# A three-block network on one core: 2 MB weight transfers in the second mixture, other queues and order in block 3

## The chip, the cores and the metric

The kernel runs on one core of one Trainium2 chip, in one launch. The metric is device time in microseconds (us), from the start to the end of one execution. Of the kernel before there are three timed runs and one profiled execution.

## The reference

Three blocks run one after the other on 512 tokens of 1024 features, in float32. Each has attention layers and then a mixture of experts or a feed-forward layer. The change touches the expert layer of block 2 and the mixer of block 3. In block 2 each of 16 experts takes the 64 tokens that score highest for it and applies a gated layer of width 2048:

```
def expert_choice_ffn(h, w_router, w_gate, w_up, w_down):
    cap = max(1, EC_FACTOR * s // N_EXPERTS_2)          # 64
    aff = jax.nn.softmax(logits, axis=-1)
    g, idx = lax.top_k(jnp.swapaxes(aff, 1, 2), cap)
    xe = h[bidx, idx]
    a = jnp.einsum('becd,edf->becf', xe, w_gate)        # 16 x [1024, 2048]
    u = jnp.einsum('becd,edf->becf', xe, w_up)          # 16 x [1024, 2048]
    ye = jnp.einsum('becf,efd->becd', jax.nn.silu(a) * u, w_down)   # 16 x [2048, 1024]
    ye = ye * g[..., None].astype(ye.dtype)
    return jnp.zeros_like(h).at[bidx, idx].add(ye)
```

So 16 experts have 24 MB of weights each, 384 MB in all (MB is 2^20 bytes here). Block 3 mixes two attentions, gated:

```
def hybrid_mixer_3(x, w_in, b_gate, ...):
    q_na, k_na, v_na, q_lat, kv_lat, k_rope, g_a, g_b = jnp.split(x @ w_in, offs, axis=-1)
    y_a = neighbourhood_attention_2d(q_na, k_na, v_na, na_rpb) @ w_branch_na
    y_b = latent_attention(q_lat, kv_lat, k_rope, ...) @ w_branch_mla
    merged = jax.nn.sigmoid(g_a + b_a) * y_a + jax.nn.sigmoid(g_b + b_b) * y_b
    return merged @ w_out
```

Both attentions have 8 heads; the latent one (MLA) attends over all 512 tokens, in four blocks of 128 queries.

## The kernel before

The kernel is written in a tile language: the program allocates tiles from pools, and a planner at build time orders each engine's instructions, queues included, by a simulated time line and puts in the waits. A pool with n buffers of a name hands them out in rotation, and a new use waits for the last reader of the old one. DMAs are issued from the queue of the engine named in the call: `nc.sync` is SyncE (SP in the profile), `nc.scalar` ScalarE (ACT), `nc.gpsimd` GpSimd (POOL). An engine's queue is worked off in order.

**The second mixture** (`moe2`, from line 1622). `lend` (line 330) builds a rotation of sixteen 1 MB buffers, [128, 2048] float32 each: 4 of the pool `rx`, the two halves of the tile `xl`, the 4 buffers `raw`, and 6 of the pool of the mixture (`rx` and the mixture's own are called `rawx` in the profile). `raw_tile` (line 323) hands out the next one; `raw_group` (line 349) issues the load on SyncE's queue (line 354). While the tokens are being chosen (line 1632), the first expert's weights are loaded as far as there is room, and three more blocks of its up matrix go into tiles that are idle then (line 1680).

Per expert, `gather` (line 1653) first collects the 64 tokens by matmuls with a one-hot matrix, for two experts at once: it writes `xe`, 8 blocks of 128 features. Then come gate and up: for each block k of 128 rows one load of 1 MB, in which each partition holds one row of 8 KB, and 4 matmuls of 512 columns (line 1701; each is two instructions in the trace). The product is transposed by TensorE (line 1726), with columns picked at a stride of 2 that matches how the down weights lie: 8 loads of 1 MB (line 1734), each partition with two neighbouring rows, 8 KB in one run, and the matmuls of line 1738. For each pair of experts the results go back to the tokens (line 1747).

**Block 3** (`mixer3`, from line 1789). The input arrives transposed and split in a high and a low part (`xh`, `xl`). `wsplit` casts each weight block on ScalarE (`wh`, line 227) and subtracts on VectorE (`wl`, line 230); each product is then three matmuls (lines 376 and 428). The values of the neighbourhood attention come first (`dense_tiles`): `ev_v` copies each of the four token tiles into the one buffer `nv` and stores it to memory (`vd`, line 1811). After queries and keys the windows of values are loaded back (`vw`, eight loads, line 1830), and per pair of heads two table rows (`rv`, line 1839). Stores, reloads and table rows are issued on ScalarE's queue. The weights for values, queries and keys come through the 4 `raw` buffers. `merged` are eight tiles for the gated sum, not yet in use at that time.

MLA comes in parts: a pair of heads `hp` and a block of queries `qt`. A part computes the scores of its two heads (line 1968), their softmax (`softmax2`), then transposes both (`transposes`, line 442), copies them out (lines 445 and 447) and multiplies with the values (line 1980), whose matmuls `together` keeps side by side. `stagger` (line 116) interleaves the parts: the second half of a part follows the first half of the next one (the first four parts) or of the second next (the other twelve).

Of the kernel before, what the change touches and what calls it, by code (L numbers as in the profile page):

```python
# [24 lines left out]
F32 = mybir.dt.float32  # L25
F32R = mybir.dt.float32r
# [9 lines left out]
P = 128  # L36
S = 512
# [90 lines left out]
class Net:  # L128
# [306 lines left out]
    def transposes(self, dst, src, nb, eng="v"):  # L435

        nc = self.nc
        for b in range(0, nb, 4):
            m = min(4, nb - b)
            pt = self.pst()  # L440
            for k in range(m):
                nc.tensor.transpose(pt[:, k * P:(k + 1) * P], src[:, (b + k) * P:(b + k + 1) * P], self.ident)  # L442
            v = pt[:, :m * P].rearrange("p (k t) -> p k t", k=m)
            if eng == "v":
                nc.vector.tensor_copy(dst[:, b:b + m], v)
            else:
                nc.scalar.copy(dst[:, b:b + m], v)

    def softmax2(self, es, sps, scale, tabs=None, sinks=None, normalize=True):
# [1172 lines left out]
    def moe2(self, after):  # L1622
        nc, tc, I = self.nc, self.tc, self.I
        aff = self.aff
        with ExitStack() as cx:
            M = cx.enter_context(tc.tile_pool(name="moe2", bufs=1, reuse_waits="tile"))
            self.lend((self.RW, 4), "xl", self.rp, (M, 6))
            wk = self.np.tile([P, S], F32, name="nx", bufs=2)
# [22 lines left out]
            hn = self.hn  # L1651

            def gather(e, g):

# [22 lines left out]
            for i, place in enumerate(places[:3]):  # L1677
                early.append(place())
                for f, t in enumerate(early[i]):
                    nc.sync.dma_start(t, I["w_exp_up_2"][0][(5 + i) * P:(5 + i + 1) * P, f * 512:(f + 1) * 512])  # L1680
            yp = ohT = None
            first = gather(0, 1)
            for e in range(16):
# [32 lines left out]
                for ab in range(2):  # L1716
# [7 lines left out]
                    for k in range(4):  # L1724
                        f = k // 2 * 256 + k % 2
                        nc.tensor.transpose(pt[:, k * P:(k + 1) * P], t[:, f:f + 255:2], self.ident)  # L1726
                    nc.scalar.copy(ut, pt.rearrange("p (k t) -> p k t", k=4))  # L1727
# [3 lines left out]
                order = [(ab, c, kk) for ab in range(2) for c in range(2) for kk in range(4)]  # L1731
                for i in range(0, 16, 2):
                    raw = self.raw_tile().rearrange("p (g n) -> p g n", g=2)
                    nc.sync.dma_start(raw, Wd[i * P:(i + 2) * P, :].rearrange("(p g) n -> p g n", g=2))
                    for d in range(2):
                        ab, c, kk = order[i + d]
                        for hf in range(2):
                            nc.tensor.matmul(py[hf * 64:(hf + 1) * 64], uT[ab][:, kk, c * 64:(c + 1) * 64],  # L1738
                                             raw[:, d, hf * 512:(hf + 1) * 512], start=(i + d == 0), stop=(i + d == 15))
                r0 = slice((e % 2) * 64, (e % 2) * 64 + 64)  # L1740
                nc.scalar.copy(yp[r0, 0:512], py[0:64])
                nc.vector.tensor_copy(yp[r0, 512:1024], py[64:128])
                if e % 2 == 1:
                    for a in range(4):
                        for hf in range(2):
# [4 lines left out]
                            nc.vector.tensor_add(o, o, pc)  # L1750
            self.cycle = None
            self.mixer3_open()
# [36 lines left out]
    def mixer3(self, after):  # L1789
# [18 lines left out]
        def ev_v(a, ps):  # L1808
            t = N.tile([P, 512], F32, name="nv")
            nc.vector.tensor_copy(t, ps)  # L1810
            nc.scalar.dma_start(vd[a * P:(a + 1) * P, :], t)

        self.dense_tiles(W, 8, 1024, 512, xh, xl, ev_v)
        anti = self.const("anti", N)
# [5 lines left out]
            q[j].rearrange("p (j r c) -> p j r c", j=4, r=8), ps.rearrange("p (r j c) -> p j r c", j=4, r=8),  # L1820
            AF.Copy, scale=0.125))
        self.dense(W, 8, 512, 512, "T", xh, xl, lambda j, ps: nc.vector.tensor_copy(k[j], ps))
        starts = (0, 8, 24, 32)
        vw = []
        for j in range(4):
            row = []
            for kk in range(2):
                t = N.tile([P, 512], F32, name=f"vw{j}{kk}")
                o = vd[(kk * 4) * 64 + starts[j]:, :]
                nc.scalar.dma_start(t, bass.AP(tensor=o.tensor, offset=o.offset, ap=[[64 * 512, 4], [512, 32], [1, 512]]))  # L1830
                row.append(t)
# [121 lines left out]
        def mla_part(hp, qt):  # L1953
# [12 lines left out]
            sp = self.sc() if hp == 0 or qt % 2 == 0 else [self.acc(), self.acc()]  # L1966
            for b in range(2):
                nc.tensor.matmul(sp[b] if isinstance(sp, list) else sp[:, b], T[2 * b][:96, qt * P:(qt + 1) * P],
                                 T[2 * b + 1][:96], start=True, stop=True)
            e = H.tile([P, 2, S], F32, name="e", bufs=3)  # L1970
# [11 lines left out]

            self.together([lambda kt=kt, b=b: values(kt, b) for kt in range(4) for b in (1, 0)])
            nc.scalar.copy(o_ml[hp][:, qt * P:(qt + 1) * P], po[:, :P])

        heads = {}
        stagger(mla_part(0, qt) for qt in range(4))
# [125 lines left out]
```

## Time and profile before

| | us |
|---|---|
| three runs | 3346.15, 3352.58, 3354.76 |
| median | 3352.58 |
| the profiled execution's own time | 3355.08 |
| its span in the profile | 3353.2 |

The page has the busy time of each engine, then the span in 40 slices (a digit is the busy share in tenths, with the DMA engines' share and GB/s below), the DMA queues, and the chain of work that ended last. Other views list instructions in order of time with the idle time before them and what ended it (in brackets), waits by engine, or busy time in given stretches. In rows of stretches the columns are: stretch, length, then busy us and number of instructions for PE, PEld, DVE, ACT and POOL, then granted TensorE clock, DMA share and GB/s. PE is TensorE, PEld its weight loads, DVE VectorE; a trailing q marks an engine's queue of DMA issues.

### The profile page before, as it was taken

The numbers are of one execution on the slowest core, as the hardware profiler recorded it, in microseconds if no ns is written. First come the engines' busy times: TensorE is split into PE (matmuls) and PEld (weight loads), VectorE is DVE, ScalarE is ACT, GpSimd is POOL, SyncE is SP. The second block draws the span as 40 slices with busy tenths as digits, with TensorE's granted clock in tenths as the row PEclk, the third lists the DMA queues.
The fourth block names the chain that finished last, engine by engine and source line by source line (L and its number), as shares of the span: only waits on it lengthen the run. The fifth ranks groups of instructions, "written<-read, shape, count | busy, mean of one in ns | idle before, by whom it ended". The sixth has DMA issues, their size and how long they took to land.

```text
span 3353.2 us, 41283 instructions
## 1 busy us (share of the span) xinstructions
PE 3168.3 (94%) x15456; PEld 2062.4 (62%) x15456; DVE 1632.4 (49%) x3520; ACT 1291.2 (39%) x2662; POOL 130.9 (4%) x128
## 2 busy tenths in 40 slices
PE   8999989998989999999999999899888999999998
PEld 6778766667758777677534333322225685788886
DVE  5557799987364444856211111011105546573356
ACT  6335568876354354654000000000003444452244
POOL 0010110001000000000000000000000000000000
PEclk9999989999999999999899999999999999999999
DMA  5115489975112122125799999999995220132243
GB/s 174 67 66 157 173 305 382 370 282 177 63 38 88 63 66 88 39 89 199 315 420 426 427 427 427 427 427 427 427 427 205 72 95 26 63 114 90 81 170 138
DMA packets 196554, 713.96 MB, mean 213 GB/s; under 512 B 20144, under 2 KB 28096, under 8 KB 147584
## 3 DMA queue, kind: packets, MB, share of 16 engines
q1 hardware_dynamic: 173888, 668.38, 51.4%
q10 hardware_dynamic: 19520, 32.43, 3.1%
q0 software_dynamic: 2944, 10.49, 1.0%
q8 instruction: 123, 2.02, 0.2%
q14 instruction: 79, 0.65, 0.1%
HBM read 693.68 MB, written 17.56 MB: 212 GB/s over the span
## 4 chain that ended last, share of the span: by engine, by line
PE 69%; DMA 15%; DVE 8%; ACT 4%; issue 2%; POOL 1%; ACTq 0%; POOLq 0%; SPq 0%; DVEq 0%
PE acc L428 23%; PE acc L291 7%; PE acc L1701 6%; PE acc L1103 5%; PE acc L1295 5%; DMA xl<-in_w_exp_up_dram 3%; DMA rawx<-in_w_exp_gate_dram 3%; PE acc L1738 3%; PE acc L1125 3%; DMA rawx<-in_w_exp_down_dram 2%; DMA xl<-in_w_exp_down_dram 2%; PE sc L1664 2%; PE acc L376 2%; PE pst L442 2%; DVE wl L230 2%
## 5 line engine op out<-in xcount | busy, mean ns | idle before, releaser
L230 DVE TENSOR_TENSOR wl<-raw,wh 128x512 fp32r<-128x512 f32 (+3 forms) x910 | 606.0, 682 | 578.6 <-ACT wh L227 528.9
L227 ACT CAST wh<-raw 128x512 fp32r<-128x512 f32 (+3 forms) x910 | 546.5, 612 | 717.1 <-PE acc L428 475.1
L428 PE MATMUL acc<-xh,wh 128*128 128x512 f32 x1072 | 426.5, 398 | 7.2 <-ACT wh L227 5.2
L428 PE MATMUL acc<-xl,wh 128*128 128x512 f32 x1072 | 424.5, 396 | 0.0
L428 PE MATMUL acc<-xh,wl 128*128 128x512 f32 x1072 | 423.1, 395 | 0.0
L1701 PE MATMUL acc<-rawx,xe 128*64 128x512 f32 x1256 | 293.1, 601 | 28.1 <-DMA rawx<-in_w_exp_up_dram 20.4
L428 PEld LDWEIGHTS acc<-xh,wh 128*128 128x128 f32 x1072 | 202.4, 189 | 57.1 <-ACT wh L227 7.8
L428 PEld LDWEIGHTS acc<-xh,wl 128*128 128x128 f32 x1072 | 202.5, 189 | 47.0 <-issue 6.7
L428 PEld LDWEIGHTS acc<-xl,wh 128*128 128x128 f32 x1072 | 202.7, 189 | 44.2 <-issue 5.6
L1701 PEld LDWEIGHTS acc<-rawx,xe 128*64 128x64 f32 x1256 | 84.4, 137 | 227.5 <-issue 149.8
L1738 PE MATMUL acc<-rawx,wh 128*64 128x512 f32 x640 | 145.9, 598 | 10.6 <-DMA rawx<-in_w_exp_down_dram 10.6
L291 PE MATMUL acc<-wl,xsh 128*128 128x512 f32 x336 | 133.8, 398 | 4.8 <-DVE wl L230 4.7
L216 POOL TENSOR_TENSOR pw_r<-pw_v,halfneg 128x1 f32<-128x1 f32 (+2 forms) x64 | 59.1, 924 | 2008.2 <-DVE pw_v L215 1990.6
L291 PE MATMUL acc<-wh,xsl 128*128 128x512 f32 x336 | 132.9, 396 | 0.0
L291 PE MATMUL acc<-wh,xsh 128*128 128x512 f32 x336 | 128.9, 392 | 0.0
L1701 PE MATMUL acc<-raw,xe 128*64 128x512 f32 x512 | 118.5, 597 | 8.4 <-DMA raw<-in_w_exp_gate_dram 8.4
L1720 DVE SCALAR_TENSOR_TENSOR wl<-wl,acc 128x512 f32<-128x512 f32 x32 | 22.0, 687 | 203.6 <-PE acc L1701 203.6
L1727 ACT COPY wh<-pst 128x512 f32<-128x512 f32 x32 | 18.8, 586 | 259.8 <-PE pst L1726 259.7
L477 ACT ACTIVATE e<-e,smx 128x512 f32<-128x512 f32 (+3 forms) x160 | 98.9, 619 | 50.2 <-DVE smx L475 36.4
L1103 PE MATMUL acc<-wh,xeh 128*96 128x512 f32 x256 | 103.7, 406 | 0.7 <-ACT xeh L227 0.7
L1738 PEld LDWEIGHTS acc<-rawx,wh 128*64 128x64 f32 x640 | 42.7, 136 | 99.2 <-issue 70.7
L1103 PE MATMUL acc<-wl,xeh 128*96 128x512 f32 x256 | 103.5, 404 | 0.1
(537 smaller groups left out, 5475.1 us busy)
## 6 DMA issues: line engine op xcount, KB each, us to landing
rawx<-in_w_exp_up_dram SPq DMA_DIRECT2D x80, 1024.0 KB
rawx<-in_w_exp_down_dram SPq DMA_DIRECT2D x80, 1024.0 KB
rawx<-in_w_exp_gate_dram SPq DMA_DIRECT2D x77, 1024.0 KB
raw<-in_w_in_dram SPq DMA_DIRECT2D x58, 1024.0 KB
raw<-in_w_exp_gate_dram SPq DMA_DIRECT2D x34, 1024.0 KB
raw<-in_w_exp_down_dram SPq DMA_DIRECT2D x32, 1024.0 KB
raw<-in_w_exp_up_dram SPq DMA_DIRECT2D x30, 1024.0 KB
raw<-in_w_ffn_out_dram SPq DMA_DIRECT2D x22, 1024.0 KB
```

The lines of the kernel that those rows point to most:

```text
L227: nc.scalar.copy(hi, src)
L230: nc.vector.tensor_sub(lo, src, hi.bitcast(F32))
L291: nc.tensor.matmul(acc[a, hf], l[:, js], r, start=(k == 0 and q == 0), stop=(k == nk - 1 and q == 2))
L376: self.nc.tensor.matmul(acc[a], l[:, k, js], r[:, :n], start=(k == 0 and q == 0), stop=(k == nk - 1 and q == 2))
L428: nc.tensor.matmul(outs[j], l, r, start=(kk == 0 and q == 0), stop=(kk == nk - 1 and q == 2))
L442: nc.tensor.transpose(pt[:, k * P:(k + 1) * P], src[:, (b + k) * P:(b + k + 1) * P], self.ident)
L477: nc.scalar.activation(es[i], src[i], AF.Exp, bias=nm[:, i:i + 1], scale=sc[i], accum_out=l[:, i:i + 1])
L1103: nc.tensor.matmul(ps, l[:, k], r, start=(k == 0 and q == 0), stop=(k == 7 and q == 2))
L1125: nc.tensor.matmul(py[hf], l[:, k], r, start=(k == 0 and q == 0), stop=(k == 3 and q == 2))
L1295: nc.tensor.matmul(acc[j], l[:, js], r, start=(k == 0 and q == 0), stop=(k == nk - 1 and q == 2))
L1701: nc.tensor.matmul(acc[f // 2][f % 2 * 64:(f % 2 + 1) * 64], cur[:, k, es], raw[f], start=(k == 0), stop=(k == 7))
L1738: nc.tensor.matmul(py[hf * 64:(hf + 1) * 64], uT[ab][:, kk, c * 64:(c + 1) * 64], raw[:, d, hf * 512:(hf + 1) * 512], start=(i + d == 0), ...
```

## The change

In the mixture, a transfer is 2 MB: 256 rows, of which partition p holds rows 2p and 2p+1 (gate and up) or 512 rows, of which it holds rows 4p to 4p+3 (down), a run of 16 KB per partition. The rotation has eight places of 2 MB in the same memory: two of `rx`, the tile `xl`, two `raw` buffers, three of the mixture's pool, two `raw` buffers. A place of two `raw` buffers is loaded by two transfers of 1 MB with 8 KB runs. The feature blocks follow: block k of the contraction is now every second feature of a group of 256 (`feature`), which is also how `gather` picks its columns, and the transposes before the down matrix pick at a stride of 4. The very last load is split in two. The block k = 4 of the first expert's up matrix is a load of its own.

In block 3 the stores of the values, their reloads and the table rows go to GpSimd's queue; the four value tiles are staged in buffers of the attention's later tiles instead of `nv`; the loads of values, queries and keys are all issued first, the keys' into the room of `merged`. MLA's parts are cut in four steps and driven by `weave`, which for the last twelve parts fixes TensorE's order: first scores, the transposes of the part two back, second scores, that part's values.

```diff
-            self.lend((self.RW, 4), "xl", self.rp, (M, 6))
+            big = lambda pool, n: lambda: [pool.tile([P, 4096], F32, name="rawx", bufs=n)]
+            xl = lambda: [self.xp.tile([P, 8, S], F32R, name="xl").bitcast(F32).rearrange("p k t -> p (k t)")]
+            one = lambda: self.rp.tile([P, 2048], F32, name="raw")
+            two = lambda: [one(), one()]
+            cycle = itertools.cycle([big(self.RW, 2)] * 2 + [xl, two] + [big(M, 3)] * 3 + [two])
+            def load(W, r0, g, parts=1):
+                n = 4096 // g
+                src = W[r0:r0 + P * g, :].rearrange("(p g) n -> p g n", g=g)
+                at = next(cycle)()
+                at = [t.rearrange("p (g n) -> p g n", n=n) for t in at]
+                if len(at) == 1 and parts > 1:
+                    at = [at[0][:, i * (g // parts):(i + 1) * (g // parts)] for i in range(parts)]
+                m = g // len(at)
+                for i, t in enumerate(at):
+                    nc.sync.dma_start(t, src[:, i * m:(i + 1) * m])
+                return [at[i // m][:, i % m] for i in range(g)]
...
+            feature = lambda k: k // 2 * 256 + k % 2
...
-                            nc.tensor.matmul(ps[:, i], hn[:, a, (m + i) * P:(m + i + 1) * P], oh[:, a],
+                            nc.tensor.matmul(ps[:, i], hn[:, a, feature(m + i):feature(m + i) + 255:2], oh[:, a],
...
-                            raw = self.raw_group(W, k, 1, 0, 2048)
-                            raw = [raw[:, 0, f * 512:(f + 1) * 512] for f in range(4)]
+                            if e == 0 and pg and k == 4:
+                                rows = [one()]
+                                nc.sync.dma_start(rows[0], W[feature(k):feature(k) + 255:2, :])
+                            elif k % 2 == 0:
+                                rows = load(W, k * P, 2)
+                            raw = [rows[k % 2][:, f * 512:(f + 1) * 512] for f in range(4)]
...
-                        nc.tensor.transpose(pt[:, k * P:(k + 1) * P], t[:, f:f + 255:2], self.ident)
+                        nc.tensor.transpose(pt[:, k * P:(k + 1) * P], t[:, k:k + 509:4], self.ident)
...
-                for i in range(0, 16, 2):
-                    raw = self.raw_tile().rearrange("p (g n) -> p g n", g=2)
-                    nc.sync.dma_start(raw, Wd[i * P:(i + 2) * P, :].rearrange("(p g) n -> p g n", g=2))
+                for i in range(0, 16, 4):
+                    raw = load(Wd, i * P, 4, 2 if (e, i) == (15, 12) else 1)
...
-        merged = [B.tile([P, S], F32, name=f"m{i}") for i in range(8)]
+        room = B.tile([P, 8, S], F32, name="m")
+        merged = [room[:, i] for i in range(8)]
...
-            t = N.tile([P, 512], F32, name="nv")
+            t = (N.tile([P, 2, 256], F32, name="ne", bufs=2).rearrange("p i k -> p (i k)") if a % 2 else
+                 N.tile([P, 4, P], F32, name="neT", bufs=2).rearrange("p k t -> p (k t)"))
             nc.vector.tensor_copy(t, ps)
-            nc.scalar.dma_start(vd[a * P:(a + 1) * P, :], t)
-        self.dense_tiles(W, 8, 1024, 512, xh, xl, ev_v)
+            nc.gpsimd.dma_start(vd[a * P:(a + 1) * P, :], t)
+        raws = {c: [self.raw_group(W, kg, 4, c, 512) for kg in (0, 4)] for c in (1024, 0)}
+        for kg in (0, 4):
+            nc.sync.dma_start(room[:, kg:kg + 4], W[kg * P:(kg + 4) * P, 512:1024].rearrange("(g p) n -> p g n", p=P))
+        raws[512] = [room[:, kg:kg + 4] for kg in (0, 4)]
+        self.dense_tiles(W, 8, 1024, 512, xh, xl, ev_v, raws=raws[1024])
...
-                nc.scalar.dma_start(t, bass.AP(tensor=o.tensor, offset=o.offset, ap=[[64 * 512, 4], [512, 32], [1, 512]]))
+                nc.gpsimd.dma_start(t, bass.AP(tensor=o.tensor, offset=o.offset, ap=[[64 * 512, 4], [512, 32], [1, 512]]))
...
-                nc.scalar.dma_start(rv, bass.AP(tensor=rpb.tensor, offset=rpb.offset + (2 * hp + hh) * 945,
+                nc.gpsimd.dma_start(rv, bass.AP(tensor=rpb.tensor, offset=rpb.offset + (2 * hp + hh) * 945,
...
+            scores(0)
+            yield
+            with behind():
+                last[0] = scores(1).ins
             e = H.tile([P, 2, S], F32, name="e", bufs=3)
             self.softmax2([e[:, b] for b in range(2)], sp, 96 ** -0.5)
             yield
             eT = H.tile([P, 2, 4, P], F32, name="eT", bufs=2)
             for b in range(2):
-                self.transposes(eT[:, b], e[:, b], 4, eng="a" if b else "v")
+                last[0] = self.transposes(eT[:, b], e[:, b], 4, eng="a" if b else "v")
+            yield
...
+            with behind():
+                self.together([lambda kt=kt, b=b: values(kt, b) for kt in range(4) for b in (1, 0)])
...
+        def weave(parts, depth, tied):
+            open_ = []
+            for g in parts:
+                o = open_.pop(0) if len(open_) == depth else None
+                next(g)
+                last[1] = tied and o is not None
+                if o is None or not tied:
+                    next(g)
+                if o is not None:
+                    next(o)
+                    if tied:
+                        next(g)
+                    next(o, None)
+                open_.append(g)
+            last[1] = False
+            for g in open_:
+                next(g)
+                next(g, None)
...
-        stagger((mla_part(hp, qt) for hp in range(1, 4) for qt in range(4)), 2)
+        weave([mla_part(hp, qt) for hp in range(1, 4) for qt in range(4)], 2, True)
```

`behind()` places what stands in it directly behind the instruction `last[0]` in TensorE's order (only in the tied parts). The first four parts are woven with depth 1 and not tied.

More of the change, by code (lines that the diff above doesn't have):

```diff
@@ L1 @@
+import itertools
 import math
@@ L441, in transposes @@
             for k in range(m):
-                nc.tensor.transpose(pt[:, k * P:(k + 1) * P], src[:, (b + k) * P:(b + k + 1) * P], self.ident)
+                mm = nc.tensor.transpose(pt[:, k * P:(k + 1) * P], src[:, (b + k) * P:(b + k + 1) * P], self.ident)
             v = pt[:, :m * P].rearrange("p (k t) -> p k t", k=m)
@@ L447, in transposes @@
                 nc.scalar.copy(dst[:, b:b + m], v)
+        return mm.ins
     def softmax2(self, es, sps, scale, tabs=None, sinks=None, normalize=True):
@@ L1679, in moe2 @@
                 for f, t in enumerate(early[i]):
-                    nc.sync.dma_start(t, I["w_exp_up_2"][0][(5 + i) * P:(5 + i + 1) * P, f * 512:(f + 1) * 512])
+                    r = feature(5 + i)
+                    nc.sync.dma_start(t, I["w_exp_up_2"][0][r:r + 255:2, f * 512:(f + 1) * 512])
             yp = ohT = None
@@ L1724, in moe2 @@
                     for k in range(4):
-                        f = k // 2 * 256 + k % 2
-                        nc.tensor.transpose(pt[:, k * P:(k + 1) * P], t[:, f:f + 255:2], self.ident)
+                        nc.tensor.transpose(pt[:, k * P:(k + 1) * P], t[:, k:k + 509:4], self.ident)
                     nc.scalar.copy(ut, pt.rearrange("p (k t) -> p k t", k=4))
@@ L1731, in moe2 @@
                 order = [(ab, c, kk) for ab in range(2) for c in range(2) for kk in range(4)]
-                for i in range(0, 16, 2):
-                    raw = self.raw_tile().rearrange("p (g n) -> p g n", g=2)
-                    nc.sync.dma_start(raw, Wd[i * P:(i + 2) * P, :].rearrange("(p g) n -> p g n", g=2))
-                    for d in range(2):
+                for i in range(0, 16, 4):
+                    raw = load(Wd, i * P, 4, 2 if (e, i) == (15, 12) else 1)
+                    for d in range(4):
                         ab, c, kk = order[i + d]
@@ L1738, in moe2 @@
                             nc.tensor.matmul(py[hf * 64:(hf + 1) * 64], uT[ab][:, kk, c * 64:(c + 1) * 64],
-                                             raw[:, d, hf * 512:(hf + 1) * 512], start=(i + d == 0), stop=(i + d == 15))
+                                             raw[d][:, hf * 512:(hf + 1) * 512], start=(i + d == 0), stop=(i + d == 15))
                 r0 = slice((e % 2) * 64, (e % 2) * 64 + 64)
@@ L1750, in moe2 @@
                             nc.vector.tensor_add(o, o, pc)
-            self.cycle = None
             self.mixer3_open()
@@ L1820, in mixer3 @@
             q[j].rearrange("p (j r c) -> p j r c", j=4, r=8), ps.rearrange("p (r j c) -> p j r c", j=4, r=8),
-            AF.Copy, scale=0.125))
-        self.dense(W, 8, 512, 512, "T", xh, xl, lambda j, ps: nc.vector.tensor_copy(k[j], ps))
+            AF.Copy, scale=0.125), raws=raws[0])
+        self.dense(W, 8, 512, 512, "T", xh, xl, lambda j, ps: nc.vector.tensor_copy(k[j], ps), raws=raws[512])
         starts = (0, 8, 24, 32)
@@ L1966, in mla_part, with scores @@
             sp = self.sc() if hp == 0 or qt % 2 == 0 else [self.acc(), self.acc()]
-            for b in range(2):
-                nc.tensor.matmul(sp[b] if isinstance(sp, list) else sp[:, b], T[2 * b][:96, qt * P:(qt + 1) * P],
-                                 T[2 * b + 1][:96], start=True, stop=True)
+            def scores(b):
+                return nc.tensor.matmul(sp[b] if isinstance(sp, list) else sp[:, b],
+                                        T[2 * b][:96, qt * P:(qt + 1) * P], T[2 * b + 1][:96], start=True, stop=True)
+            scores(0)
+            yield
+            with behind():
+                last[0] = scores(1).ins
             e = H.tile([P, 2, S], F32, name="e", bufs=3)
@@ L1981, in values, with behind @@
                                         start=(kt == 0), stop=(kt == 3))
-            self.together([lambda kt=kt, b=b: values(kt, b) for kt in range(4) for b in (1, 0)])
+            with behind():
+                self.together([lambda kt=kt, b=b: values(kt, b) for kt in range(4) for b in (1, 0)])
             nc.scalar.copy(o_ml[hp][:, qt * P:(qt + 1) * P], po[:, :P])
         heads = {}
-        stagger(mla_part(0, qt) for qt in range(4))
+        last = [None, False]
+        def behind():
+            return tc.issue_after(last[0]) if last[1] else ExitStack()
+        def weave(parts, depth, tied):
[16 more added lines that the diff above has]
+                next(g, None)
+        weave([mla_part(0, qt) for qt in range(4)], 1, False)
         for hf in range(2):
```

## The prediction, made before the change was run

> **What bounds the kernel now.** I read the page first, then the chain of waits through the second mixture, the DMA queues and the stretches of busy time there, and after it the time lines of TensorE and ScalarE in block 3. The page:
>
> ```profile
> span 3353.2 us, 41283 instructions
> ...
> DMA  5115489975112122125799999999995220132243
> GB/s 174 67 66 157 173 305 382 370 282 177 63 38 88 63 66 88 39 89 199 315 420 426 427 427 427 427 427 427 427 427 205 72 95 26 63 114 90 81 170 138
> ```
>
> A slice is 83.8 us. From slice 21 to slice 30 the DMA engines are full at 427 GB/s: that is the second mixture. The chain inside it (start, length, what):
>
> ```profile
> 1863.32 17.34 PE acc L1701 x80
> 1880.68 17.56 DMA rawx<-in_w_exp_gate_dram
> ...
> 2504.77 19.56 DMA raw<-in_w_exp_down_dram
> 2524.47 1.95 PE acc L1738 x8
> ```
>
> Until 1880 the chain runs over TensorE, from there to 2524 mostly over loads. TensorE is then always waiting for the next load, down to the last one:
>
> ```profile
> 2507.20 1.94 PE L1701 MATMUL acc<-rawx,xe 128*64 128x512 f32 x8 [0.51 <-DMA rawx<-in_w_exp_up_dram]
> ...
> 2531.76 1.94 PE L1738 MATMUL acc<-rawx,wh 128*64 128x512 f32 x8 [0.54 <-DMA rawx<-in_w_exp_down_dram]
> ```
>
> 1.94 us of work per 1 MB, of 2.45 us between loads. So the mixture ends when its bytes have landed: what counts is the rate of the stream, and when it became continuous. Block 3 after it is bound by TensorE, with holes that I cost below.
>
> **The rate of the stream.** What does a longer run save? The queue rows of a stretch with 8 KB packets only (1800 to 2300), and of one with mostly 2 KB packets (579 to 583):
>
> ```profile
> DMA packets 29280, 213.38 MB, mean 427 GB/s; under 512 B 3250, under 2 KB 3250, under 8 KB 3250
> q1 hardware_dynamic: 29259, 213.08, 100.9%
> ```
>
> ```profile
> q1 hardware_dynamic: 627, 1.25, 80.3%
> ```
>
> Let a packet cost a fixed p and each MB cost b of engine time. The first gives 29259 p + 213.08 b = 1.009 x 16 x 500 = 8072 us, the second 627 p + 1.25 b = 0.803 x 16 x 4 = 51.4 us. So p = 8.9 ns (8.5 to 9.3 by the rounding of 1.25) and b = 36.7 us. The 3250 small packets are the 16 completion writes of each transfer. A 1 MB transfer is then 8 data packets and 1 small one per engine, two of them 18 packets; one 2 MB transfer with 16 KB runs is 9. It saves 9 x 8.9 = 80 ns of 4.97 us. Of the eight places in the new rotation six take 2 MB whole and two stay split in 1 MB with 8 KB runs, so 16 MB save 6 x 80 = 0.48 us. The stream is full from 1680 (windows below) to 2531.8, 852 us; 16 MB take 39.3 us at 427 GB/s, so that is 21.7 times 0.48: **-10 us**. No row shows a 16 KB load from memory; the ends are 0 (a run is cut in 8 KB packets and only completions fall away) and -13 (all eight places). I take -10, since the two rows lie on one line of which 16 KB is the continuation.
>
> [...]
>
> TensorE has 0.5 us idle per MB to let the stream run faster, so nothing takes its place. The strided gather and transposes lie in the same cover; were it gone (before 1880), they would still only move the point where TensorE catches up with the loads. The last load is split in two, so the tail behind it stays 1.94 us.
>
> **The start of the stream.** Buffers keep their 16 MB, in 8 places instead of 16.
>
> ```profile
> 1600.00:1620.00 20.00, 19.27 (x60) 9.34 (x59) 5.90 (x11) 0.85 (x2) 0.00 (x0) 0.57 0.42 170
> 1620.00:1640.00 20.00, 20.00 (x107) 9.38 (x107) 0.87 (x3) 0.53 (x2) 0.00 (x0) 1.00 0.81 302
> 1640.00:1660.00 20.00, 20.00 (x99) 7.74 (x99) 3.44 (x5) 2.63 (x5) 0.00 (x0) 1.00 0.97 381
> 1660.00:1680.00 20.00, 20.00 (x123) 11.00 (x120) 2.58 (x4) 0.58 (x1) 0.00 (x0) 1.00 0.90 363
> 1680.00:1700.00 20.00, 20.00 (x96) 6.68 (x94) 1.37 (x2) 1.19 (x2) 0.00 (x0) 1.00 1.01 426
> ```
>
> The last column but one is the DMA share. Against 1.01 the stream loses (0.59 + 0.20 + 0.04 + 0.11) x 20 = 18.8 us here, because every place is full until TensorE frees it. TensorE begins the first expert at 1612 and frees a place per k of some 3.8 us:
>
> ```profile
> 1622.25 1.89 PE L1701 MATMUL acc<-rawx,xe 128*64 128x512 f32 x8
> ...
> 1626.06 1.89 PE L1701 MATMUL acc<-rawx,xe 128*64 128x512 f32 x8
> ```
>
> A 2 MB place comes free only after its second k, one step of 3.81 us later; since the frees still come in pairs and the lost time is made up of many such steps, I take **+3 us**, nearly one step. Ends: -5 (completion and queueing happen to pack better) and +13: if SyncE's queue stands at the half place that needs the buffer of the first expert's k = 6, freed near 1639, then the engines idle from 1608 (0.42 of 20 us into that window) to 1639, 31 us instead of 18.8. [...]
>
> **Block 3, the value loads.** Stores of the values, their reloads and the table rows leave ScalarE's queue for GpSimd's. ScalarE and TensorE at that place:
>
> ```profile
> 2574.90 10.52 ACTq L1830 DMA_DIRECT2D vw<-vd  x3
> 2585.51 0.62 ACT L227 CAST wh<-raw 128x512 fp32r<-128x512 f32 x1 [10.02 <-DMA vw<-vd]
> ...
> 2593.70 2.18 ACT L227 CAST wh<-raw 128x512 fp32r<-128x512 f32 x4 [7.56 <-issue]
> ```
>
> ```profile
> 2586.19 0.50 PE L428 MATMUL acc<-xh,wh 128*128 128x512 f32 x1 [0.30 <-ACT wh L227]
> ...
> 2594.37 0.80 PE L428 MATMUL acc<-xh,wh 128*128 128x512 f32 x1 [4.88 <-ACT wh L227]
> ...
> 2600.08 0.46 PE L428 MATMUL acc<-xl,wh 128*128 128x512 f32 x1
> ```
>
> ```profile
> 2597.00:2600.00 3.00, 3.00 (x8) 2.32 (x7) 0.00 (x0) 0.54 (x1) 0.00 (x0) 0.50 1.03 255
> ```
>
> ScalarE stands behind its own DMA issues, the casts behind it are late, TensorE runs dry: 0.30 + 4.88 us. Then it runs at half clock (0.50 in the window): the 13 matmuls from 2594.37 to 2600.08 take 5.71 us, 0.44 each, at full clock half of that, so 2.8 more. Together **-8 us**. Next in line is TensorE itself: the cast takes 0.62 us of a step of 12 matmuls, which at 0.22 each is 2.6 us. GpSimd's price for such a DMA is not shown; its nearest row is an indirect one:
>
> ```profile
> 425.76 2.40 POOL L1132 DMA_INDIRECT xe<-hn_d,rt  x1 [10.40 <-DVE rt L1078]
> ...
> L1876 PE MATMUL pst<-neT,vw x128: 272/273/324, 2630.6 to 2684.8; 128*64 128x128 f32 x128
> ```
>
> Four stores, eight reloads and two table rows at 2.4 us are 34 us on GpSimd's queue, from 2560 to 2594; the first reader (L1876) is at 2630, 8 us earlier then: 28 us of cover. GpSimd's own work (the powers of the norms) lies before the values and behind the attention, so nobody waits for its queue meanwhile. Without the cover, each us late would be one lost. The early loads of three column blocks, and the values' four staging tiles, I cost at nothing: TensorE waits for ScalarE there, not for a load. Range of the part: -8 to 0.
>
> **Block 3, latent attention.** The order of the first four parts is as before. For the other twelve it becomes: scores of head 0, transposes of the part two back, scores of head 1, its values. Now (group, then time line):
>
> ```profile
> L1980 PE MATMUL acc<-eT,mv 128*64 128x128 f32 x192 | 17.7, 293 | 7.1 <-ACT eT L447 7.1
> ```
>
> ```profile
> 2859.36 0.43 PE L1980 MATMUL acc<-eT,mv 128*64 128x128 f32 x2 [0.73 <-ACT eT L447]
> ...
> 2861.80 1.12 PE L1968 MATMUL acc<-mkT,mqT 96*128 96x512 f32 x2
> 2862.76 1.04 PE L442 MATMUL pst<-c_ident,e 128*128 128x128 f32 x8
> 2863.64 1.02 PE L1968 MATMUL sc<-mkT,mqT 96*128 96x512 f32 x2
> 2864.59 1.09 PE L1980 MATMUL acc<-eT,mv 128*64 128x128 f32 x16
> 2865.61 1.13 PE L1968 MATMUL sc<-mkT,mqT 96*128 96x512 f32 x2
> ```
>
> Every other part has a hole of 0.7 us between transposes and values; where scores stand between (2863.64, 0.95 us) there is none. The new order puts scores there each time. Three of the ten holes lie in the last parts, which have no scores left: 7/10 of 7.1 is **-5 us**. The new danger is the transposes' own wait: from a part's second scores to its transposes there are three more scores, two groups of values and one of transposes, 3 x 0.95 + 2 x 1.02 + 0.88 = 5.8 us. Its softmax takes 5.0:
>
> ```profile
> 2857.79 1.23 DVE L465 TENSOR_REDUCE smx<-sc 128x2 f32<-128x1024 f32 x1 [1.28 <-PE sc L1968]
> ...
> 2861.68 0.88 DVE L485 TENSOR_SCALAR e<-e,smx 128x512 f32<-128x512 f32 x2
> ```
>
> (2857.6 to 2862.6.) It fits with 0.8 us to spare. Range -7 to 0 without a rival's turn.
>
> **Sum**: -10 + 3 - 8 - 5 = -20 us against the profiled execution's 3355.1, so 3335; that execution lies 2.5 us above the median of the three runs, 3352.6, on which I put the forecast: **3333 us**. A measurement tells about 0.3%, 10 us, from no change.
>
> **Rivals.** (1) A run of 16 KB goes no faster, because it is cut in 8 KB packets or memory serves it slower: -10, 3343. For it: no such packet in the trace. Against it: the line through 2 KB and 8 KB. 0.13. (2) SyncE's queue stands at the half place: +13 instead of +3, 3343. For it: the 18.8 us that the start already loses; against it: the half place can be queued later. 0.10. (3) Slower: the fixed order makes TensorE wait in each part of the latent attention, and its clock drops to half there. These windows show the drop and its absence:
>
> ```profile
> 2814.00:2817.00 3.00, 1.57 (x2) 0.84 (x3) 1.86 (x7) 2.72 (x8) 0.00 (x0) 0.71 0.00 0
> 2817.00:2820.00 3.00, 3.00 (x8) 1.56 (x7) 1.58 (x3) 0.00 (x0) 0.00 (x0) 0.50 0.02 5
> ...
> 2870.00:2880.00 10.00, 7.81 (x78) 5.72 (x76) 5.21 (x12) 4.14 (x12) 0.00 (x0) 1.00 0.00 0
> ```
>
> 1.4 us idle of 3 halved it; 22% idle over 10 us did not. A part has 3.8 us of matmuls, so it decides between 1.1 us of wait per part (22%) and 3.5 (47%). The price: ten parts at twice 3.8 us, +38, and the 5 not won: 3333 + 43 = 3376. Against it: 0.8 us to spare in the softmax. 0.07. (4) More: the start packs better (-5, 8 below my term) and the half clock near 2815 vanishes (about 6 us): 3319. 0.08.
>
> **How the numbers follow.** The forecast has 0.62. Faster by over 0.3%: 0.62 + 0.08 and a third of rivals 1 and 2 (0.08), with 0.04 taken off for small misses: 0.74. Same: the rest of these two and the misses, 0.18. Slower: rival 3 and 0.01, 0.08. The range is 3317 to 3346: from rival 4 to rivals 1 and 2 with 3 us on top; it leaves out rival 3 and both rivals together.
>
> **What would show it.** Right: GB/s of 430 to 432 in the full stretch, with half as many data packets; the last load some 7 us earlier than 2531.8; no idle row at L428 after ScalarE near 2590 and a clock of 1.00 there; L1980's idle near 2 us. Wrong: 427 GB/s still; a DMA hole of over 25 us between 1600 and 1680; idle before L442 that DVE ends; TensorE waiting for vw or the table rows.

## The result and the profile after

| | us |
|---|---|
| before, four runs: median (range) | 3352.76 (3346.15 to 3354.76) |
| after, four runs: median (range) | 3329.97 (3328.95 to 3330.21) |
| ratio, 95% interval | 0.9935, 0.9918 to 0.9952 |
| the profiled execution after: its time, its span | 3330.21, 3328.4 |

The forecast was 3333 in a range of 3317 to 3346. The sum was right, and its terms were not: the experiments below show two of them too large, one half as large as it should be, and one of the right size that comes to nothing without steps which I had costed at nothing.

The page of the kernel after, its span and the slices to hold against those of before:

```profile
span 3328.4 us, 41050 instructions
...
DMA  5115489985112212115799999999997321133253
GB/s 174 63 65 160 166 303 382 370 295 189 54 51 76 64 66 89 51 64 193 284 423 418 429 430 429 429 431 429 429 429 279 83 73 49 64 115 99 73 171 139
```

The full stretch now moves 429 to 431 GB/s, where it was 427. But the second full slice has 418, a dip that before did not have. The queue row of 1800 to 2300, then the stretch with the dip:

```profile
q1 hardware_dynamic: 18463, 214.47, 100.6%
```

```profile
1760.00:1790.00 30.00, 29.93 (x163) 14.29 (x164) 2.63 (x4) 1.75 (x3) 0.00 (x0) 1.00 0.98 391
```

Fewer packets by over a third, 0.65% more bytes: 5.5 us of the 852. In the 30 us of the dip 391 GB/s instead of 430 lose 2.7 us. SyncE stood in this stretch up to 8.1 us at one load, waiting for TensorE's line 1730 (before: 3.5 us at most). That eight large places come free in larger steps than sixteen small ones would explain this; it is read from the waits and not shown by a run of its own. The start itself lost nothing: the five windows of 20 us from 1600 to 1700 moved 128, 289, 403, 410 and 414 GB/s, 1644 in all, before 1642. The end of the stream, TensorE's time line:

```profile
2518.39 3.60 PE L1765 MATMUL acc<-raw,wh 128*64 128x512 f32 x16
2524.24 8.78 PE L1765 MATMUL acc<-rawx,wh 128*64 128x512 f32 x32 [2.25 <-DMA rawx<-in_w_exp_down_dram]
```

Before, TensorE followed the loads in steps of 1.94 us. Now it waits 2.25 us for a 2 MB load and then has 32 matmuls in one lump, which absorbs the last load too: the last down matmul ends at 2533.0, before at 2533.7.

In block 3 the stretch where ScalarE stood behind its DMA issues is full, at clock 1.00 (before: 9.19 and 5.63 us busy of 10, the second at a clock of 0.67):

```profile
2580.00:2590.00 10.00, 10.00 (x46) 8.28 (x45) 2.39 (x4) 2.54 (x5) 2.71 (x4) 1.00 1.04 243
2590.00:2600.00 10.00, 10.00 (x46) 8.28 (x45) 2.46 (x4) 4.07 (x8) 0.00 (x0) 1.00 0.35 95
```

In the latent attention the value matmuls wait 2.1 us in all, where it was 7.1, and they are busy for 13.1 us instead of 17.7:

```profile
L2019 PE MATMUL acc<-eT,mv 128*64 128x128 f32 x192 | 13.1, 279 | 2.1 <-ACT eT L448 2.1
```

For all kernels below I cut three stages out of TensorE's time line. The mixture runs from its first gate matmul to the end of its last down matmul; the middle stage from there to the transposes of the second pair of heads (those that wait 0.23 or 0.24 us for mqT); the latent attention from these to the first matmul of the projection behind it. Start and end of that last stage in the kernel after:

```profile
2798.91 0.64 PE L1993 MATMUL pst<-c_ident,qn 128*96 128x128 f32 x4 [0.23 <-ACT mqT L1995]
...
2855.93 0.50 PE L1297 MATMUL acc<-wh 128*128 128x512 f32 x1
```

| kernel | mixture | middle | latent attention |
|---|---|---|---|
| before | 921.5 | 274.3 | 72.7 |
| after | 920.1 | 265.9 | 57.0 |
| mixture only | 921.0 | 275.0 | 66.6 |
| values only | 921.7 | 267.0 | 68.3 |
| latent attention only | 921.6 | 274.4 | 58.7 |
| 2 MB, 8 KB runs | 924.1 | 275.1 | 72.7 |
| 2 MB, 4 KB runs | 934.5 | 274.7 | 66.6 |
| queue only | 921.3 | 276.1 | 69.5 |
| last expert split | 919.4 | 266.6 | 57.0 |
| block 3 only, twice | 920.7, 921.6 | 267.2, 267.0 | 57.0, 58.7 |
| after, again | 921.3 | 265.9 | 58.7 |
| order untied | 920.9 | 265.9 | 66.6 |
| filler matmuls | 921.3 | 274.6 | 66.6 |

So between the two profiled executions 1.4 us come from the mixture, 8.4 from the middle and 15.7 from the latent attention.

### The profile page after: what moved, and what is told of

Same layout as the page of the kernel before. It is cut to its first block, busy times and chain, and to the rows that moved or that the text cites. A ratio compares the mean times of both kernels' runs of the same rounds, so it can differ in the third digit from the quotient of the medians.

```text
span 3328.4 us, 41050 instructions
## 1 busy us (share of the span) xinstructions
PE 3150.4 (95%) x15456; PEld 2075.4 (62%) x15456; DVE 1635.3 (49%) x3520; ACT 1290.3 (39%) x2662; POOL 143.5 (4%) x148
## 4 chain that ended last, share of the span: by engine, by line
PE 71%; DMA 13%; DVE 9%; ACT 4%; issue 2%; POOL 1%; ACTq 0%; POOLq 0%; SPq 0%; DVEq 0%
PE acc L429 24%; PE acc L292 7%; PE acc L1730 7%; PE acc L1105 5%; PE acc L1297 5%; DMA rawx<-in_w_exp_up_dram 5%; PE acc L1765 4%; PE acc L1127 3%; DMA raw<-in_w_exp_down_dram 3%; PE sc L1688 2%; DMA rawx<-in_w_exp_gate_dram 2%; PE acc L377 2%; DMA rawx<-in_w_exp_down_dram 2%; ACT e L479 2%; PE pst L443 2%
## 5 line engine op out<-in xcount | busy, mean ns | idle before, releaser
L231 DVE TENSOR_TENSOR wl<-raw,wh 128x512 fp32r<-128x512 f32 (+1 forms) x902 | 601.5, 683 | 573.6 <-ACT wh L228 524.6
L228 ACT CAST wh<-raw 128x512 fp32r<-128x512 f32 (+1 forms) x902 | 541.7, 611 | 705.1 <-PE acc L429 466.6
L217 POOL TENSOR_TENSOR pw_r<-pw_v,halfneg 128x1 f32<-128x1 f32 (+2 forms) x64 | 58.7, 918 | 1898.8 <-DVE pw_v L216 1881.4
```

What stands on the lines that cost most here:

```text
L228: nc.scalar.copy(hi, src)
L231: nc.vector.tensor_sub(lo, src, hi.bitcast(F32))
```

## The experiments

### The three parts alone

Each takes one part of the change and leaves the rest as before: the loads and rotation of the mixture; the queues, early loads and staging of the values; `weave` with its fixed order.

```diff
-            self.lend((self.RW, 4), "xl", self.rp, (M, 6))
+            cycle = itertools.cycle([big(self.RW, 2)] * 2 + [xl, two] + [big(M, 3)] * 3 + [two])
```

> The mixture's part of the change alone (2 MB transfers, 16 KB runs, permuted blocks); block 3 as before. Theory read from the two traces: the stream runs at 430 instead of 427 GB/s (5.5 us over 852 us), but a hole near 1770 (2 to 2.5 us) and a last 2 MB load whose 32 matmuls come in one lump (1.8 us) give most of it back: the last down matmul ends near 2533, the time is 0 to 2 us below the kernel before (3351 to 3353). Rival, the forecast's own terms: -10 for the rate and +3 for the start, so 7 below (3346) and the last down matmul near 2527.

Measured: 3347.37 against 3351.54 of before on the same chip, ratio 0.9987 (0.9978 to 0.9996): 4.4 us less, 1.3 to 7.4. The time lies between the two theories. The trace follows the first: 430 GB/s, the dip (398 GB/s from 1760 to 1790), the lump, the last down matmul ending at 2534.0 and a mixture only 0.5 us shorter than before. The runs without a profile gained more than that; I come back to it below.

```diff
-            nc.scalar.dma_start(vd[a * P:(a + 1) * P, :], t)
+            nc.gpsimd.dma_start(vd[a * P:(a + 1) * P, :], t)
...
+        self.dense_tiles(W, 8, 1024, 512, xh, xl, ev_v, raws=raws[1024])
```

> The queues and early loads around the neighbourhood attention alone; mixture and latent attention as before. Theory: each gain belongs to its place, so the 0.30 + 4.88 us of idle time and the half clock after it go, 8.4 us (3344). Rival: the half clock near 2815 in the latent attention (6.8 us) belongs to the moment at which that stage is entered and not to the order of its matmuls; then an entry 8.4 us earlier can remove it too, 15 us in all (3337).

Measured: 3344.56, ratio 0.9979 (0.9969 to 0.9988): 7.0 us less. The middle stage is 7.3 us shorter. The first theory holds.

```diff
-        stagger((mla_part(hp, qt) for hp in range(1, 4) for qt in range(4)), 2)
+        weave([mla_part(hp, qt) for hp in range(1, 4) for qt in range(4)], 2, True)
```

> The new order of the latent attention alone; mixture and values as before. Theory: the whole 15.7 us that this stage lost in the traces belong to the order (the holes at the value matmuls, the tighter steps, and no half clock near 2815): 3337. Rival 1: the half clock there depends on the moment of entry, which is as before here: 15.7 less 6.8, 9 us (3344). Rival 2, the forecast: only the holes, 5 us (3348).

Measured: 3341.23, ratio 0.9968 (0.9956 to 0.998): 10.7 us less, 6.7 to 14.7. That is nearest to rival 1, and the forecast's 5 us lie outside. Rival 1's reason, the moment of entry, is not shown by it: the stage begins within 0.2 us of before (2808.22 and 2808.04). The stage takes 58.7 us, the 57.0 of after and 1.7 for a stretch of half clock near 2815. That stretch came and went with the old order too. The same two windows, in the kernel before, with the mixture alone, and with the values alone, three kernels with the same order there:

```profile
2810.00:2820.00 10.00, 8.19 (x17) 3.48 (x17) 6.19 (x13) 2.79 (x8) 0.00 (x0) 0.76 0.01 2
2820.00:2830.00 10.00, 8.80 (x33) 4.86 (x31) 4.25 (x10) 2.69 (x8) 0.00 (x0) 0.56 0.00 0
```

```profile
2810.00:2820.00 10.00, 7.20 (x25) 3.43 (x26) 7.16 (x15) 3.63 (x10) 0.00 (x0) 1.00 0.01 3
2820.00:2830.00 10.00, 9.05 (x63) 5.49 (x63) 5.95 (x14) 5.01 (x13) 0.00 (x0) 1.00 0.00 0
```

```profile
2810.00:2820.00 10.00, 8.65 (x42) 4.82 (x40) 6.43 (x15) 3.85 (x11) 0.00 (x0) 0.83 0.01 2
2820.00:2830.00 10.00, 8.99 (x63) 5.50 (x62) 5.28 (x11) 4.57 (x13) 0.00 (x0) 1.00 0.00 0
```

In windows of 1 us the kernel before reads 1.00 up to 2815, 0.50 from 2816 to 2828 and 1.00 from 2829, with 0.62 and 0.56 in the two windows between. With these two levels, taken for the others too, a window mean of c over 10 us is 20 x (1 - c) us at half clock: 13.6 us in the first, none in the second, 3.4 in the third, all after the same idle time of 1.81 us. The stage takes 72.7, 66.6 and 68.3 us accordingly. So 6.1 of the 15.7 us between the two profiled executions belong to that one execution before, and 9.6 (66.6 to 57.0) are the order's.

The three parts by their ratios are 4.4, 7.0 and 10.7 us, 22.1 together; the whole change is 21.8. They add up.

### What the mixture's 4 us are made of

The same transfers of 2 MB, places and waits, with each partition's 16 KB in two runs of 8 KB and then in four of 4 KB:

```diff
-                src = W[r0:r0 + P * g, :].rearrange("(p g) n -> p g n", g=g)
+                src = W[r0:r0 + P * g, :]
+                src = (src.rearrange("(h p) n -> p h n", h=2) if g == 2 else
+                       src.rearrange("(h p g) n -> p h (g n)", h=2, g=2))
```

```diff
+                src = W[r0:r0 + P * g, :].rearrange("(h p) (c n) -> p c h n", h=g, n=1024)
```

> As the mixture alone, with the same 2 MB transfers, places and waits, but each partition's 16 KB in two runs of 8 KB from different rows, and the contraction blocks of the kernel before. Theory: the run length makes the rate, so it is 427 to 428 GB/s again (only half of the completion packets go, 8.9 ns of 4.97 us) and the mixture ends some 4 us later than with 16 KB runs; time 3354 to 3358, above the kernel before, since hole and lump stay. Rival: the rate comes from the number of transfers, not of the runs: 430 GB/s and the time of the mixture alone.

> As the 2 MB transfers with 8 KB runs, but in runs of 4 KB: the same transfers, places and waits, and 16 data packets more per engine and 2 MB. Theory: a fixed cost per packet. By the forecast's 8.9 ns these are 142 ns of 4.9 us (2.9%): 415 GB/s and 25 us more than with 8 KB runs, 3378. By the 7.0 ns that the rows of 8 and 16 KB give: 112 ns, 417 GB/s, 20 us, 3373. [...]

Measured: 3353.09 with 8 KB, ratio 1.0007 (0.9998 to 1.0016), and 3363.08 with 4 KB, ratio 1.0033 (1.002 to 1.0045). The data queue from 1800 to 2300, 8 KB runs and then 4 KB runs:

```profile
q1 hardware_dynamic: 28063, 213.25, 100.9%
```

```profile
DMA packets 49336, 210.85 MB, mean 422 GB/s; under 512 B 2009, under 2 KB 2009, under 8 KB 45220
...
q1 hardware_dynamic: 49316, 210.55, 102.0%
```

For 8 KB the first theory holds: at the transfers' new size, but with the old runs, the rate is the old one. 2 MB, 2.097 million bytes, take 500 x 2.097/213.25 = 4.917 us. With 16 KB runs (214.47) it is 4.889, with 4 KB runs 4.980. By the same rows 2 MB are 276.0 packets with 8 KB runs, 180.5 with 16 KB and 491.2 with 4 KB, over 16 engines 17.2, 11.3 and 30.7. (With 16 KB two of the eight places stay at 8 KB runs; with 4 KB these two do for gate and up, so the 16 packets more that I expected are 13.4 on the mean.) So 13.4 more packets per engine cost 63 ns, 4.7 ns each; and 16 KB runs, which save 6.0, save 28 ns, also 4.7 each. For 4 KB both of my prices are refuted: they gave 415 and 417 GB/s and 25 and 20 us, the rate is 422 GB/s, and the two medians lie 10.0 us apart (10.4 the two mixtures, 8.7 by the two ratios).

Run length, from 8 to 16 KB and with the order of the feature blocks that goes with it, is 3353.09 - 3347.37 = 5.7 us by the medians and 3.1 by the two mixtures (924.1 and 921.0); the larger places and transfers give back 3353.09 - 3351.54 = 1.5 us by the medians, not distinguishable from zero, and 2.6 by the traces (924.1 against 921.5).

The lump at the end can be taken away:

```diff
-                    raw = load(Wd, i * P, 4, 2 if (e, i) == (15, 12) else 1)
+                    raw = load(Wd, i * P, 4, 2 if e == 15 else 1)
```

> The changed kernel with all four loads of the last expert's down matrix split in two transfers of 1 MB (8 KB runs), instead of the last load alone. Theory: the mixture's end is late because the last but one 2 MB load lands in one lump, so TensorE has 32 matmuls (8.78 us) left after it; with halves it follows the loads, the last down matmul ends near 2530.7 instead of 2533.0, and the time is 2 to 2.5 us below the changed kernel's. Rival: the end is set by the landing of the last byte, whatever the pieces: no gain.

Measured: 3327.41, ratio to before 0.9934 (0.9921 to 0.9948), beside 3330.53 for the changed kernel on the same chip. The end of its stream:

```profile
2525.87 1.94 PE L1765 MATMUL acc<-rawx,wh 128*64 128x512 f32 x8 [0.41 <-DMA rawx<-in_w_exp_down_dram]
2528.32 1.94 PE L1765 MATMUL acc<-rawx,wh 128*64 128x512 f32 x8 [0.52 <-DMA rawx<-in_w_exp_down_dram]
2530.78 1.94 PE L1765 MATMUL acc<-rawx,wh 128*64 128x512 f32 x8 [0.53 <-DMA rawx<-in_w_exp_down_dram]
```

TensorE follows the loads again. In the trace the mixture is 1.5 us shorter than the mean of the four others with its rotation and runs (920.2, 921.0, 921.3, 920.9), not 2 to 2.5. It has the lowest median of all kernels here, but its five runs (3325.02 to 3330.57) overlap those of after.

Most of what the lump costs is clock. 32 such matmuls in one piece, from the kernel before; then the last lump's window in the kernel after, and the same window in the split one:

```profile
1705.11 7.04 PE L1738 MATMUL acc<-raw,wh 128*64 128x512 f32 x32
```

```profile
2520.00:2530.00 10.00, 7.75 (x30) 2.71 (x28) 0.00 (x0) 0.00 (x0) 0.00 (x0) 0.83 1.01 413
```

```profile
2520.00:2530.00 10.00, 8.92 (x40) 2.40 (x36) 0.00 (x0) 0.00 (x0) 0.00 (x0) 1.00 1.02 411
```

At a clock of 1.00, as in the first of these views, the lump would take 7.04 us, not 8.78. A mean of 0.83 over 10 us is 3.4 us at half clock (windows of 1 us read 0.57, 0.50, 0.50 and 0.72 from 2525 to 2529, and 1.00 before and behind), so 1.7 us lost, close to the 1.5 that splitting gains. All six traces with the lump show the 8.78 us, after a wait of 2.24 to 2.75 us, and the four of them with a window there a clock of 0.83; of the eight whose end goes in steps of 1.94 us, after waits near 0.5 us, the six with a window there have 1.00. No run keeps the lump and the full clock, so the two are not told apart by experiment.

> The change without its mixture: 1 MB transfers and the old rotation, with both changes of block 3. Its distance to the changed kernel is what the mixture's part is worth where block 3 is the new one. Theory: the traces put 0 to 1 us on it, so this kernel takes 3330 to 3332. Rival: the 4.2 us by which the mixture alone was below the kernel before are the mixture's own: 3334. The forecast: 7 us, 3337.

> The changed kernel once more, unchanged, beside the two above on one chip: 3328 to 3332 if the four runs so far are typical. Where the half clock in the latent attention is a matter of the moment, some runs show it: 1.7 us or more above the rest, at a clock lower by 0.0005 per 1.7 us.

> The change without its mixture once more, since its five runs lay between 3330 and 3336: the mixture's part by the medians is 3.8 us there, by the traces 0.5 us. Theory 1: the medians are right, since the profiled executions of the kernels with 2 MB transfers lie at the slow end of their runs: 3333 to 3335 again. Theory 2: the traces are right: 3330 to 3331.

Measured, without the mixture's part (before's loads, both changes of block 3): 3334.35, ratio 0.9955 (0.9942 to 0.9969), and once more 3332.34, ratio 0.9937 (0.9925 to 0.9949). The changed kernel again: 3330.53, ratio 0.9942 (0.9928 to 0.9955). The 3332.34 lies between the two theories of the repeat. All eleven runs of the one have the median 3332.57, all nine of the other 3330.18, on more than one chip: 2.4 us. Beside the new block 3 the mixture's part is thus worth 2 to 4 us by the medians, and the intervals of the ratios overlap. The traces see 0.4 to 0.5. The repeat of the changed kernel loses 1.7 us to half clock in its latent attention (58.7 instead of 57.0; 0.89 and 0.94 in the windows from 2800 to 2820), as was thought possible. The profiled executions with 2 MB transfers lay high among the runs of their kernel (the slowest of 4, second slowest of 11, second slowest of 5, the slowest of 5 and of 11, but the fourth of 7), those with 1 MB transfers did not, but for the one of before. Whether recording itself disturbs the larger transfers, these runs can't tell.

### Why the middle stage gains

```diff
-            nc.scalar.dma_start(vd[a * P:(a + 1) * P, :], t)
+            nc.gpsimd.dma_start(vd[a * P:(a + 1) * P, :], t)
...
-                nc.scalar.dma_start(t, bass.AP(tensor=o.tensor, offset=o.offset, ap=[[64 * 512, 4], [512, 32], [1, 512]]))
+                nc.gpsimd.dma_start(t, bass.AP(tensor=o.tensor, offset=o.offset, ap=[[64 * 512, 4], [512, 32], [1, 512]]))
```

> The kernel before with one thing changed: the stores of the values, their reloads and the table rows are issued on GpSimd's queue. The loads of values, queries and keys and the staging buffer nv are as before. Theory (the forecast's): ScalarE behind its own DMA issues was the whole cause, so the 8 us come with the queue alone: 3342 to 3345, no idle row at L428 near 2590 after ScalarE. Rival: with the casts no longer late, the next thing late is a load (the weights of queries and keys wait for the four raw buffers) or the store through the one nv: 0 to 4 us of gain, and TensorE idle there behind a DMA or nv.

Measured: 3352.58, ratio 0.9999 (0.999 to 1.0007). My theory falls, the rival holds. ScalarE's stall is gone, and TensorE waits longer than before, at another place. What is written to and read from the staging tile nv, and VectorE's copies into it:

```profile
its engine sat idle before it (us, times) until:
...
  DMA vd<-nv: 8.4, 1
who waited for it (us, times):
...
  PE acc L428: 7.5, 1
...
DMA to landing us min/median/max: 2.4/2.6/11.5
```

```profile
2563.85 0.69 DVE L1810 COPY nv<-acc 128x512 f32<-128x512 f32 x1
2577.33 0.69 DVE L1810 COPY nv<-acc 128x512 f32<-128x512 f32 x1 [8.45 <-DMA vd<-nv]
```

Half of the stores land within 2.6 us. One takes 11.5: reloads and a table row, now issued right beside it, share the DMA engines with it (their share is 1.06 from 2566 to 2570). nv is one buffer, so VectorE waits 8.45 us for that landing, and TensorE 7.51 us for VectorE's copy. So the queue alone gains nothing, and with four staging buffers and the early loads it gains 7.0 us. That it is the staging that was missing is read from this trace: the staging and the early loads were not tried one by one, nor without the queue.

### Why the fixed order gains

```diff
-        weave([mla_part(hp, qt) for hp in range(1, 4) for qt in range(4)], 2, True)
+        weave([mla_part(hp, qt) for hp in range(1, 4) for qt in range(4)], 2, False)
```

> The changed kernel with the same four steps of each part of the latent attention, but without the fixed order of TensorE. Theory: the fixed order makes the gain, so TensorE falls back to the order of before, ten holes of 0.7 us at the value matmuls come back and the stage takes 66.6 us (more with a half clock) instead of 57. Rival: the cut into steps is enough: 57 to 59 us.

Measured: one run, 3342.23; the stage takes 66.6 us at a clock of 1.00. The theory holds: cut in four steps, but with the planner free, TensorE's order is the old one. (The switch also hands the planner both scores of a part one after the other again, so the run does not tell that sequence from the binding of the matmuls to each other.) The old order at full clock, in the kernel with the mixture alone (group, then time line):

```profile
L2005 PE MATMUL acc<-eT,mv 128*64 128x128 f32 x192 | 16.5, 281 | 7.1 <-ACT eT L448 7.1
```

```profile
2839.84 1.04 PE L443 MATMUL pst<-c_ident,e 128*128 128x128 f32 x8
2841.56 0.43 PE L2005 MATMUL acc<-eT,mv 128*64 128x128 f32 x2 [0.68 <-ACT eT L448]
2841.92 1.13 PE L1993 MATMUL acc<-mkT,mqT 96*128 96x512 f32 x2
2842.97 1.09 PE L2005 MATMUL acc<-eT,mv 128*64 128x128 f32 x14
```

and the new order, in the kernel after:

```profile
2839.13 1.04 PE L443 MATMUL pst<-c_ident,e 128*128 128x128 f32 x8
2840.01 1.02 PE L2001 MATMUL acc<-mkT,mqT 96*128 96x512 f32 x2
2840.96 1.09 PE L2019 MATMUL acc<-eT,mv 128*64 128x128 f32 x16
```

A hole costs more than its 0.68 us of idle time. After it two of the sixteen value matmuls run by themselves, 0.43 us, and the other fourteen still take the 1.09 us that all sixteen take in one piece. Busy time falls by 16.5 - 13.1 = 3.4 us, idle time by 7.1 - 2.1 = 5.0; of the rest of the 9.6, busy time of scores and transposes is 0.7. (Busy times of neighbouring groups overlap a little, in the last view above by 0.07 us at 2840.96, so these parts need not add up.)

```diff
+            if (hp, qt) == (1, 2):
+                warm = self.pst()
+                for _ in range(2):
+                    nc.tensor.matmul(warm, T[0][:96, :P], T[1][:96], start=True, stop=True)
```

> The kernel before with two more 128x512 matmuls (their product is not used) ahead of the scores for which TensorE waits 1.81 us in the latent attention (sc, released by ScalarE's e). Theory: that idle time is what drops the clock there, for 13.6 us in the profile of before (6 us lost), 3.4 or nothing in others; filled, the clock stays at 1.00 from 2800 to 2880, the stage takes 66.6 to 67 us instead of 68.3 to 72.7, the median falls by 3 to 6 us and the spread of the runs (3345 to 3358 before) narrows. Rival 1: the drop belongs to something else in the stage (the two waits for mqT, the holes at the values): the half clock still comes, and the time stays within 1 us of before. Rival 2: the extra matmuls lengthen the path: up to 2 us more.

Measured: 3349.66 against 3349.70, ratio 1.0 (0.9991 to 1.0009). In its trace the idle time and the half clock are gone:

```profile
2810.00:2820.00 10.00, 9.22 (x28) 3.92 (x26) 7.18 (x15) 3.80 (x10) 0.00 (x0) 1.00 0.01 2
```

The stage takes 66.6 us, as the theory gave, but the median does not move, which it did not give: either the long half clock of the profiled execution before is not what most runs have, or the two matmuls do not remove it in most. One such trace can't prove the cause, since other traces show no half clock with the idle time in place.

## Why the prediction was right in sum and wrong in its terms

**The rate of the stream, -10.** Its direction and cause were right, its size was not: run length is worth 5.7 us by the medians and 5.5 by the rate. The step that failed is the price of a packet, "p = 8.9 ns", which took the time that packets spent as time that the engines lost: measured by throughput, it is 4.7 ns. Where the queue's share is over 100% (100.6 to 102.0% in these rows), packets overlap: from 8 to 4 KB the packets' own time per byte rose by 2.4% (102.0/210.55 against 100.9/213.25), the throughput fell by only 1.3%. In the short stretch from which the price came (579 to 583) a second queue took another 24.1% of the engines' time, 104.4% with the 80.3, which the working left out.

**The start of the stream, +3.** Nothing was lost at the start. The larger places go with a dip near 1770 and the lump at the end, with its half clock, instead: 1.5 us by the medians, 2.6 by the traces. "The tail behind it stays 1.94 us" was wrong: I split the last load in thought and forgot the whole one in front of it. With the -10 above, the mixture was put at -7 and is -4.4 alone, 2 to 4 by all medians.

**The values, -8.** Right in size, 7.0 alone. GpSimd took 0.56 to 0.72 us per issue, far below the 2.4 that I had allowed, and its cover was never used. But the failed step was: "The early loads of three column blocks, and the values' four staging tiles, I cost at nothing". With neither of them the term is zero, and the trace puts that down to the one staging buffer. I named ScalarE's stall, and did not ask what would be late behind it in the one buffer.

**Latent attention, -5.** The idle part was exact: seven tenths of 7.1 us were to go, and 7.1 became 2.1. What was missed is the broken run of matmuls behind each hole, so the order is worth 9.6 us in the traces and 10.7 by the ratio. The transposes did not wait (0.0 us idle), and rival 3 did not come. The rule behind it, that 1.4 us idle of 3 halve the clock, does not always hold: the same wait, 1.81 us, left the clock at 1.00 in the kernel with the mixture alone.

**The rivals.** 16 KB runs go faster (4.889 us per 2 MB instead of 4.917), so rival 1 fell; so did rival 2, whose hole at the start isn't there. Rival 4's half clock did vanish between the two profiled executions, but the same order has shown it long, short and not at all.

The forecast came out 3 us from the result because the mixture's 2.6 us and the values' 1.0 too much and the latent attention's 5.7 us too little partly cancel. That is luck.

## What to carry to other kernels

Price a packet by the throughput of a full queue, not by the time that its packets took: here 4.7 ns against 8.9, since the packets overlap (100.9% of the engines' time in one queue). When a stall is to go, name the next buffer and the next wait behind it, and change both in one step. A hole in front of a group of matmuls cost here its idle time, 0.68 us, and also the 0.43 us in which two of the matmuls ran by themselves, while the other fourteen still took the 1.09 us of all sixteen: so look at the busy time of a group beside its idle time. Before the last 2 MB lump the reader waited 2.25 us instead of 0.5, and the mean clock of the 10 us around that wait was 0.83: so look at the clock behind such waits as well.

## What the runs showed of the hardware

The half clock near 2815 lasted 0, 3.4, 6.8 or 13.6 us after the same 1.81 us of idle time (none with the mixture alone, 3.4 with the values alone, 6.8 with the queue alone, windows of 0.81 and 0.85, and 13.6 in the kernel before). In the mixture the last 2 MB lump has 3.4 us of half clock in the kernel after, after 2.25 us of idle time. The mean clock of a run of before goes with its time: of the 28 runs of before on one chip, those at 0.985 took 3344.90 to 3349.69 us, those at 0.981 3357.65 and 3357.72. In which stage these runs had their half clock, they do not show.

In the run with the queue alone a store of 256 KB landed after 2.4 us in the best case and after 11.5 us beside four reloads, a table row and a weight load.
